# An output product whose second pass reuses the first pass's split weights, in a fused RWKV-7, pooling and MLP decoder step

## The chip, the core and the metric

The kernel runs on one NeuronCore of a Trainium2 chip. The metric is the device time of one execution in microseconds, from the program's start to its end; 1776.5 us is the median of three runs before the change (1774.28 to 1776.87). Engines are written as the profile writes them: PE is the matrix engine and PEld its weight load, DVE the vector engine, ACT the scalar engine, POOL GpSimd, and SP the engine that only issues DMAs and semaphore operations here. DMAs are issued from the queues of SP, ACT and POOL, and each queue issues in order: a DMA that waits for data holds what stands behind it on that queue.

## What is computed

One layer of a decoder trunk over 1088 tokens (1024 of a prompt, 8 sequences of 8), with 1024 features. Cut to what matters here:

```python
h = rms_norm(x, norm_mix) * (1 + sc) + sh            # sc, sh, gt = silu(c) @ w_ada_mix + b
P = h @ w_in
o_r = rwkv7_branch(P[:, :1792]); o_p = pool_branch(P[:, 1792:2304])
g_r, g_p = split(sigmoid(P[:, 2304:]))
merged = g_r * (o_r @ w_br_rwkv) + g_p * (o_p @ w_br_pool)     # the branch sums
x = x + gt * (merged @ w_out)                                   # the output product
sh, sc, gt = split(silu(c) @ w_ada_mlp + b_ada_mlp)             # the mixer's conditioning
h = rms_norm(x, norm_mlp) * (1 + sc) + sh
x = x + gt * (square(relu(h @ w_ff1)) @ w_ff2)                  # the channel mixer
y = rms_norm(x, norm_final)
```

## The kernel before

Features lie on the 128 partitions and tokens along the free dimension: a row tile is 128 x 1088, and the 1024 features are eight such rows. The tokens are cut into three chunks of 364, 362 and 362 (CH); the first two together are 726 columns (CUT).

**Products in three parts.** Every product is made in a reduced-precision format (fp32r) from values split into a high and a low part: `mm3` multiplies high by high, high weight by low input, low weight by high input, all into one PSUM tile. So each weight half, 128 x 512 elements, has to be split as well. `weights` (L157) does this: it loads the raw half into one of two `wraw` buffers with a DMA on SP (L164), copies it to `whi` with rounding on ACT (L167), and subtracts on DVE or, for every second half, on POOL, to make `wlo` (L168). In phase 2 there are four buffers each for `whi` and `wlo` (two in the pool wp, two in p2), and weight halves are requested four ahead.

**Jobs and recording.** A `Job` is one output row of 128 features: it has weight halves, chunks, PSUM tags and a `consume` function that takes each PSUM tile off. `products` walks through the jobs in the order of a list. PE executes exactly in the order in which instructions are recorded. `Pace` decides this order: its clock advances by an estimate for each matmul recorded, the product stream is the background, and generators such as the norm or the conditioning are in front; a generator yields a number (so many ns of that clock later) or a condition. On ACT, DVE, POOL and SP the order is that of a list scheduler, which follows the dependencies, the number of buffers, and its own estimates of time.

**Phase 2** is what the change touches. In the order of recording:

- *Branch sums*, eight jobs `or_job` (L1238): one half each, all three chunks. `begin` loads two rows from DRAM scratch on ACT's queue: `t` (the gate, L1244) and `u` (the other branch's product, L1245). `consume` multiplies the gate with PSUM on DVE (L1246); `after` adds `u` on POOL (L1250), copies the high part on ACT (L1253), and makes the low part on DVE (L1254) into the tiles `ma` (726 columns) and `mb` (362). `t` and `u` share four buffers.
- *Residual rows*: `x_load` (L1264) loads the eight rows of x into `hx` buffers with DMAs on ACT's queue (L1268). It stands behind the branch sums in the list, but its loads depend only on free buffers.
- *Output product*, two passes of eight jobs `out_job` (L1271) with two halves each: the first pass over the first two chunks, the second over the third. Each pass loads and splits all 16 halves of `w_out`. `consume` is `residual` (L1428): it adds gate times PSUM to the residual row on DVE (L1433), and for the sample tokens with a second DVE operation and one on POOL (L1436, L1438).
- *The mixer's conditioning*, `ada` (L1232), a generator in front: three groups of `ada_part` (L239), each of which loads eight weight tiles of 512 KB (`hid`, four buffers, DMA on SP, L249), multiplies them on PE in four groups 7000 ns of the clock apart, and spreads the result. The first group comes 15000 + 7000 ns after the start of phase 2.
- *The mixer's norm*, `norm2` (L1278), another generator: it starts when `ada` is done. For each pass it squares the updated residual rows on ACT (L1290), adds them on DVE (L1292), takes statistics on PE (`stats`, PSUM tag wc), spreads the inverse root (`rms`), and scales the rows (L1303 to L1310, using DVE, ACT and POOL) into `ma` and `mb` again. Its temporary rows come from the four `t` buffers. The statistics are recorded 3500 ns after the seventh and the eighth output job of a pass.
- *The mixer*, `ff1_job` and `ff2_jobs`: the first three ff1 jobs run on the first two chunks as soon as the first pass is normed, then on the third chunk, and the rest on all three.

The `hx` pool has 16 row buffers. In phase 2 they hold, in turn, the branches' inputs, then the residual rows and the mixer's hidden rows.

## Time and profile before

| | |
|---|---|
| median of three runs | 1776.5 us (1774.28 to 1776.87) |
| profiled execution | 1773.06 us, span of its instructions 1771.3 us |
| PE / DVE / ACT / POOL busy | 1690.8 / 853.1 / 556.0 / 243.3 us |
| granted clock of PE, mean | 0.983 |
| moved to and from HBM | 138.64 MB read, 38.84 MB written |

The profile comes from one execution. Times in its rows are microseconds from the start of the span. A row of the timeline gives start, duration, engine, line, operation, the names of what is written and read, shape and count of merged instructions; in brackets stands how long the engine had been idle before it and what released it. L148 is the line of the helper that records every matmul, so the names of its tiles tell the products apart: `mm<-hx` and `w<-hx` belong to the branches, `mm<-ma` and `w<-mb` first to the output product and later to the mixer, `wc<-hid` to the conditioning, `wc<-kct,t` to the statistics. L168 is the split of a weight half. A group's row gives the count, then busy time and mean ns of one, then the idle time before it.

### The profile page before, as it was taken

The page shows a single profiled execution, that of the slowest core. Times are in us where ns is not written, and L with a number is a line of the kernel's source. Part 1 is how long each engine was busy: PE and PEld are TensorE (multiplying, and loading weights), DVE is VectorE, ACT ScalarE, POOL GpSimd, SP SyncE. Part 2 cuts the span into 40 slices and gives each one's busy share as a digit, 9 for nine tenths or more (in the row PEclk, how much of TensorE's full clock was granted, in tenths as well). Part 3 has the DMA queues.
Part 4 walks back from the last instruction along what each step waited for, and adds up shares of the span by engine and source line. Part 5 has one row for each costly group of instructions (what it writes and reads, how often), then busy time and mean ns, then how long its engine had stood idle before and what let it go on. Part 6 is the DMA issues. An engine that isn't in the chain of part 4 may idle for free.

```text
span 1771.3 us, 32564 instructions
## 1 busy us (share of the span) xinstructions
PE 1690.8 (95%) x13705; PEld 1581.4 (89%) x13705; DVE 853.1 (48%) x1566; ACT 556.0 (31%) x1116; POOL 243.3 (14%) x315
## 2 busy tenths in 40 slices
PE   5899999989999999998999999999999999999997
PEld 2889878877888798888889899999999999999996
DVE  5575557735673637343535742433333343323346
ACT  4433343444334334221224630303121222212132
POOL 0110101000000000002413511110111111111111
PEclk9999999989999999999999999999999999999998
DMA  8214314222413241848742221111111111111112
GB/s 334 103 64 141 136 46 152 73 93 79 135 65 116 90 138 51 319 159 321 280 168 73 83 66 48 42 48 43 47 43 42 49 42 47 43 48 42 42 42 102
DMA packets 80083, 179.61 MB, mean 101 GB/s; under 512 B 16480, under 2 KB 23136, under 8 KB 79936
## 3 DMA queue, kind: packets, MB, share of 16 engines
q1 hardware_dynamic: 72128, 156.66, 26.0%
q10 hardware_dynamic: 7664, 20.42, 3.4%
q8 instruction: 108, 1.77, 0.4%
q0 software_dynamic: 144, 0.44, 0.1%
q14 instruction: 39, 0.32, 0.1%
HBM read 138.64 MB, written 38.84 MB: 100 GB/s over the span
## 4 chain that ended last, share of the span: by engine, by line
PE 87%; DVE 6%; DMA 3%; ACT 2%; issue 2%; POOL 0%; DVEq 0%; SPq 0%; ACTq 0%; POOLq 0%
PE mm L148 58%; PE w L148 24%; PE wc L148 4%; PE w L155 1%; DMA t<-d_th 1%; DMA hx<-in_xT 1%; DVE wlo L168 0%; DVE sq L365 0%; DMA x<-in_xT 0%; DVE hv L762 0%; DVE ma L1305 0%; DMA wt<-d_x 0%; DMA aw<-in_w_ada_mix 0%; DVE hx L1423 0%; DMA hid<-in_w_ada_mlp 0%
## 5 line engine op out<-in xcount | busy, mean ns | idle before, releaser
L148 PE MATMUL mm<-hx,whi 128*128 128x362 f32 (+2 forms) x2608 | 684.3, 344 | 8.4 <-DVE t L1246 5.8
L148 PEld LDWEIGHTS mm<-hx,whi 128*128 128x128 f32 x2608 | 458.8, 192 | 44.4 <-issue 24.6
L148 PE MATMUL mm<-hx,wlo 128*128 128x362 f32 (+3 forms) x1304 | 430.8, 330 | 2.7 <-DVE wlo L168 2.7
L167 ACT ACTIVATE whi<-wraw 128x512 fp32r<-128x512 f32 x246 | 155.2, 631 | 543.6 <-PE w L148 360.1
L148 PE MATMUL mm<-ma,whi 128*128 128x364 f32 (+1 forms) x1280 | 319.1, 330 | 0.8 <-DVE ma L1254 0.5
L148 PEld LDWEIGHTS mm<-hx,wlo 128*128 128x128 f32 x1304 | 250.6, 192 | 3.4 <-DVE wlo L168 3.3
L148 PEld LDWEIGHTS mm<-ma,whi 128*128 128x128 f32 x1280 | 227.0, 189 | 8.1 <-issue 5.9
L168 DVE TENSOR_TENSOR wlo<-wraw,whi 128x512 fp32r<-128x512 f32 x157 | 115.0, 733 | 215.7 <-ACT whi L167 207.4
L148 PE MATMUL mm<-ma,wlo 128*128 128x364 f32 (+1 forms) x640 | 211.0, 330 | 0.2 <-DVE wlo L168 0.2
L168 POOL TENSOR_TENSOR wlo<-wraw,whi 128x512 fp32r<-128x512 f32 x89 | 118.1, 1327 | 658.5 <-ACT whi L167 658.5
L1433 DVE SCALAR_TENSOR_TENSOR hx<-mm,aq,hx 128x364 f32<-128x364 f32 (+4 forms) x136 | 74.7, 587 | 206.4 <-PE mm L148 206.3
L148 PE MATMUL w<-mb,whi 128*128 128x362 f32 x640 | 157.9, 328 | 0.9 <-DVE rs L1436 0.6
L148 PEld LDWEIGHTS mm<-ma,wlo 128*128 128x128 f32 x640 | 121.0, 189 | 0.5 <-DVE wlo L168 0.5
L148 PEld LDWEIGHTS w<-mb,whi 128*128 128x128 f32 x640 | 112.9, 189 | 1.5 <-issue 0.8
L1327 DVE TENSOR_TENSOR ft<-ft 128x362 f32<-128x362 f32 (+1 forms) x96 | 53.0, 575 | 127.2 <-ACT ft L1326 126.8
L148 PE MATMUL w<-mb,wlo 128*128 128x362 f32 x320 | 104.8, 328 | 1.5 <-DVE wlo L168 1.3
L148 PE MATMUL w<-hx,whi 128*128 128x362 f32 x416 | 102.9, 328 | 0.0
L148 PE MATMUL mm<-hid,whi 128*128 128x364 f32 (+4 forms) x304 | 75.3, 330 | 0.0
L148 PEld LDWEIGHTS w<-hx,whi 128*128 128x128 f32 x416 | 73.1, 189 | 0.8 <-issue 0.8
L1326 ACT ACTIVATE ft<-mm 128x364 f32<-128x364 f32 x64 | 29.3, 474 | 128.1 <-PE mm L148 128.0
L148 PE MATMUL w<-hx,wlo 128*128 128x362 f32 x208 | 67.4, 324 | 0.0
L148 PEld LDWEIGHTS w<-mb,wlo 128*128 128x128 f32 x320 | 60.6, 189 | 2.1 <-DVE wlo L168 2.1
(301 smaller groups left out, 2088.4 us busy)
## 6 DMA issues: line engine op xcount, KB each, us to landing
wraw<-in_w_ff SPq DMA_DIRECT2D x134, 256.0 KB, 2.6
wraw<-in_w_in SPq DMA_DIRECT2D x68, 256.0 KB, 2.9
hid<-in_w_ada_mlp SPq DMA_DIRECT2D x24, 512.0 KB, 5.3
d_th<-px SPq DMA_DIRECT2D x22, 544.0 KB, 3.1
wt<-d_x SPq DMA_DIRECT2D x20, 544.0 KB, 4.3
t<-d_th ACTq DMA_DIRECT2D x16, 544.0 KB, 6.5
aw<-in_w_ada_mix SPq DMA_DIRECT2D x16, 512.0 KB, 6.8
wraw<-in_w_out SPq DMA_DIRECT2D x32, 256.0 KB, 2.7
```

The source lines that it names most:

```text
L148: return self.nc.tensor.matmul(out, lhsT, rhs, **kw)
L155: self.nc.tensor.transpose(out, in_, ident)
L167: nc.scalar.activation(hi, raw, AF.Copy)
L168: (nc.gpsimd if n % 2 and n >= self.solo else nc.vector).tensor_tensor(lo, raw, hi.bitcast(F32), op=ALU.subtract)
L1326: nc.scalar.activation(t[:, :n], ps[:, :n], AF.Relu)
L1327: nc.vector.tensor_tensor(t[:, :n], t[:, :n], t[:, :n], op=ALU.mult)
L1433: nc.vector.scalar_tensor_tensor(x[:, c0:c0 + m], ps[:, :m], gt[:, 0:1], x[:, c0:c0 + m], op0=ALU.mult, op1=ALU.add)
```

## The change

Three things change in phase 2.

1. *Weights of the output product.* In the first pass the halves of the jobs 0 to 3 are split as before, and both parts are also stored to DRAM scratch (`d_w`) by DMAs on SP. The halves of the jobs 4 to 7 are split into `hx` buffers by a new function, always on DVE, and stay there. The second pass runs over the jobs in the order 4, 5, 6, 7, 0, 1, 2, 3: the first four use the parts kept, the last four load both parts back from DRAM into `whi` and `wlo`. Nothing of `w_out` is split a second time. `norm2` follows the same order in its second pass.
2. *Residual rows.* Instead of `x_load`, each branch job loads one residual row at its end. A one-column copy on POOL from the job's sum into the row (`behind`) makes the load wait for that sum. The halved gate that `x_load` also made is made ahead of the jobs.
3. *Conditioning.* `ada` starts when branch job 1 is recorded, its first two tiles wait for that job's sum through `behind`, and the lead before its first group is 12000 instead of 15000.

```diff
@@ weights @@
-    def weights(self, src):
+    def weights(self, src, keep=None):
...
+        if keep is not None:
+            for t, s in ((hi, keep[:, 0:512]), (lo, keep[:, 512:1024])):
+                nc.sync.dma_start(s, t.bitcast(F32))
...
+    def split(self, t, src):
+
+        nc = self.nc
+        raw = self.wp.tile([P, 512], F32, tag="wraw", bufs=WB[0], name=self.nm("wraw"))
+        nc.sync.dma_start(raw, src)
+        hi, lo = t[:, 0:512], t[:, 512:1024]
+        nc.scalar.activation(hi, raw, AF.Copy)
+        nc.vector.tensor_tensor(lo, raw, hi.bitcast(F32), op=ALU.subtract)
+        return [(hi[:, q * 128:(q + 1) * 128], lo[:, q * 128:(q + 1) * 128]) for q in range(4)]
+
+    def weights_again(self, src):
+
+        n = self.nw
+        self.nw += 1
+        wp, x = (self.p2, "x") if n % 4 > 1 else (self.wp, "")
+        hi = wp.tile([P, 512], F32R, tag="whi" + x, bufs=WB[1], name=self.nm("whi"))
+        lo = wp.tile([P, 512], F32R, tag="wlo" + x, bufs=WB[1], name=self.nm("wlo"))
+        for t, s in ((hi, src[:, 0:512]), (lo, src[:, 512:1024])):
+            self.nc.sync.dma_start(t.bitcast(F32), s)
+        return [(hi[:, q * 128:(q + 1) * 128], lo[:, q * 128:(q + 1) * 128]) for q in range(4)]
...
@@ stream @@
-                W[id(j), h] = self.weights(j.halves[h])
+                w = j.halves[h]
+                W[id(j), h] = w() if callable(w) else self.weights(w)
...
@@ run @@
+            self.d_w = scratch("d_w", 8)
...
@@ phase2 @@
+        def behind(x):
+
+            nc.gpsimd.tensor_copy(x[:, 0:1], self.mark[:, 0:1])
+            return x
+
         def ada():
             asb = self.row(p, "R", 1, w=9 * 128)[:, :512]
+            yield lambda: ("or_job", 1) in self.done
+            first = [behind, behind]
+
+            def tile():
+                t = self.row(p, "hid", 4)[:, :1024]
+                return first.pop()(t) if first else t
+
             for g in range(3):
-                yield from self.ada_part("w_ada_mlp", g, lambda: self.row(p, "hid", 4)[:, :1024], asb, self.aq, "b_mlp", (8 * g, 8 * g + 4), 7000, 3000, 15000 if g == 0 else 0)
+                yield from self.ada_part("w_ada_mlp", g, tile, asb, self.aq, "b_mlp", (8 * g, 8 * g + 4), 7000, 3000, 0 if g else 12000)
...
+                self.mark = t
+                x = HX(F32)
+                self.xr.append(x)
+                nc.scalar.dma_start(behind(x), io["xT"][m])
+                self.done.add(("or_job", m))
...
-        def x_load():
-            nc.vector.tensor_scalar(gt, self.am[:, 16:24, :], 0.5, None, op0=ALU.mult)
-            for m in range(8):
-                self.xr.append(HX(F32))
-                nc.scalar.dma_start(self.xr[m], io["xT"][m])
-            yield
+        nc.vector.tensor_scalar(gt, self.am[:, 16:24, :], 0.5, None, op0=ALU.mult)
+        kept = {}
+        again = (4, 5, 6, 7, 0, 1, 2, 3)
+
+        def out_half(m, i, h):
+            src, put = io["w_out"][m][:, h * 512:(h + 1) * 512], self.d_w[2 * (m % 4) + h]
+            if i:
+                return kept[m, h] if m > 3 else self.weights_again(put)
+            if m < 4:
+                return self.weights(src, put)
+            kept[m, h] = self.split(HX(), src)
+            return kept[m, h]
...
-            return Job([io["w_out"][m][:, h * 512:(h + 1) * 512] for h in range(2)], lambda: self.residual(self.xr[m], gt[:, m, :]), ch,
+            return Job([lambda h=h: out_half(m, i, h) for h in range(2)], lambda: self.residual(self.xr[m], gt[:, m, :]), ch,
...
@@ norm2 @@
-                for m in range(8):
+                for n, m in enumerate(again if i else range(8)):
                     yield lambda: ("out", m, i) in self.done
-                    t = T() if m else acc
+                    t = T() if n else acc
                     nc.scalar.activation(t[:, a:b], self.xr[m][:, a:b], AF.Square)
-                    if 0 < m < 7:
+                    if 0 < n < 7:
                         nc.vector.tensor_tensor(acc[:, a:b], acc[:, a:b], t[:, a:b], op=ALU.add)
-                    if m > 5:
+                    if n > 5:
                         yield 3500
-                        self.stats(po, acc if m == 6 else t, bl, m == 6, m == 7)
+                        self.stats(po, acc if n == 6 else t, bl, n == 6, n == 7)
...
@@ the list @@
-        order += [(x_load, 0)]
         for i in range(2):
-            for m in range(8):
+            for m in again if i else range(8):
                 order += U(out_job(m, i))
```

## The prediction

> **What bounds the kernel now.** I read the page first, then busy time by stretch around the output product, then the rows of the engines inside those stretches. The page:
>
> ```profile
> span 1771.3 us, 32564 instructions
> ...
> PE 1690.8 (95%) x13705; PEld 1581.4 (89%) x13705; DVE 853.1 (48%) x1566; ACT 556.0 (31%) x1116; POOL 243.3 (14%) x315
> ```
>
> TensorE (PE) is the bound almost everywhere, so what can be won is PE idle time, and no edit removes a matmul. Busy time by stretch, branch sums to mixer (columns: stretch, its length, then busy time and count on PE, weight load, DVE, ACT, POOL, then granted clock, DMA share, GB/s):
>
> ```profile
> 803.00:818.00 15.00, 15.00 (x92) 14.75 (x90) 2.21 (x4) 1.90 (x3) 2.21 (x2) 1.00 1.00 369
> 818.00:824.00 6.00, 0.19 (x2) 0.17 (x2) 0.82 (x2) 0.00 (x0) 0.36 (x1) 0.70 1.02 410
> 824.00:859.00 35.00, 35.00 (x206) 31.80 (x207) 20.59 (x30) 9.73 (x17) 17.82 (x9) 0.95 0.92 325
> 859.00:877.00 18.00, 17.16 (x106) 14.48 (x106) 12.81 (x15) 5.75 (x10) 9.67 (x4) 1.00 0.79 280
> 877.00:940.00 63.00, 63.00 (x391) 55.51 (x389) 20.00 (x29) 15.74 (x23) 9.02 (x7) 1.00 0.43 144
> 940.00:986.00 46.00, 40.38 (x249) 38.58 (x247) 32.93 (x48) 24.32 (x40) 21.53 (x18) 1.00 0.27 86
> ```
>
> PE is idle for 5.81 us in the second row, 0.84 us in the fourth (18.00 - 17.16) and 5.62 us in the last (46.00 - 40.38). The PE rows that place this:
>
> ```profile
> 807.48 0.50 PE L148 MATMUL mm<-hx,whi 128*128 128x364 f32 x2
> ...
> 808.97 0.49 PE L148 MATMUL mm<-hx,whi 128*128 128x364 f32 x2
> ...
> 823.86 0.95 PE L148 MATMUL mm<-hx,whi 128*128 128x364 f32 x2 [5.81 <-DVE t L1246]
> 824.60 0.51 PE L148 MATMUL mm<-hx,wlo 128*128 128x364 f32 x1
> ...
> 827.30 0.33 PE L148 MATMUL mm<-hx,wlo 128*128 128x364 f32 x1
> ...
> 835.99 1.06 PE L148 MATMUL wc<-hid,sT 128*32 128x512 f32 x8
> ...
> 866.87 0.49 PE L148 MATMUL mm<-ma,whi 128*128 128x364 f32 x2
> ...
> 939.94 0.96 PE L148 MATMUL wc<-kct,R 128*128 128x18 f32 x8
> ...
> 981.86 0.49 PE L148 MATMUL mm<-ma,whi 128*128 128x364 f32 x2
> 982.59 0.43 PE L148 MATMUL mm<-ma,wlo 128*128 128x364 f32 x1 [0.24 <-DVE wlo L168]
> 986.21 0.83 PE L148 MATMUL wc<-kct,t 128*128 128x3 f32 x6 [3.19 <-DVE t L1292]
> ```
>
> Nine matmuls take 1.49 us (807.48 to 808.97), so a branch job of 36 takes 5.96 and the first began at 806.0. After the 5.81 us wait the clock is low: nine take 2.70 (824.60 to 827.30), 1.2 too many, and the two before them 0.74 (823.86 to 824.60), 0.4 too many. The first output pass begins at 866.87, the conditioning's last group runs at 939.94; the mixer's product begins at 981.86 and stands at 986.21 for the second statistics. The chain of waits says why the first wait is there:
>
> ```profile
> 803.49 9.14 DMA hx<-in_xT
> ...
> 812.65 10.43 DMA t<-d_th
> ```
>
> The branch sums' first row is issued when a residual row has landed and takes 10.43 us behind them.
>
> **The change, part by part. Residual rows.** They go behind the sums, one per job, so the first four sum rows meet empty queues. I take the 5.81 us and the 1.6 of slow clock after it as gone: PE needs job 0's row used by job 2's start, at 817.9. After its matmuls a sum takes these steps:
>
> ```profile
> 823.18 0.98 DVE L1246 SCALAR_TENSOR_TENSOR t<-t,mm 128x364 f32<-128x364 f32 x2 [8.01 <-DMA t<-d_th]
> ```
>
> ```profile
> 825.70 2.51 POOL L1250 TENSOR_TENSOR t<-t,t 128x1088 f32<-128x1088 f32 x1 [7.33 <-DMA t<-d_th]
> ```
>
> ```profile
> 828.24 0.81 ACT L1253 ACTIVATE ma<-t 128x726 fp32r<-128x726 f32 x1 [11.24 <-POOL t L1250]
> ```
>
> ```profile
> 875.48 0.92 DVE L1254 TENSOR_TENSOR ma<-t,ma 128x726 fp32r<-128x726 f32 x1 [3.24 <-ACT ma L1253]
> ```
>
> With a third piece of 0.5 and handovers of 0.1 to 0.2 that is 5.9 us. The ten POOL copies that order the loads are one column wide; no row shows one. They lie between 0 and the 2.51 us of the 1088 columns, in width far nearer to 0, and POOL was busy for 17.8 of 35 us: nothing. Behind such a load on ACT stands the split of the same sum's last third, which waits for the same POOL addition; I take nothing, and at most 2.5 us on the last sum, which other loads outweigh below.
>
> What the move may cost is bandwidth later. Issues from 795 to 880 (count, size, median us to landing), the landing times of all sum rows, and a weight half:
>
> ```profile
> t<-d_th ACTq DMA_DIRECT2D x16, 544.0 KB, 6.5
> hid<-in_w_ada_mlp SPq DMA_DIRECT2D x14, 512.0 KB, 6.7
> hx<-in_xT ACTq DMA_DIRECT2D x8, 544.0 KB, 9.7
> ```
>
> ```profile
> DMA to landing us min/median/max: 2.7/3.9/10.4
> ```
>
> ```profile
> wraw<-in_w_out SPq DMA_DIRECT2D x32, 256.0 KB, 2.7
> ```
>
> From the first sum (806.0 + 5.96 + 1.5 + 2.5 = 816) to the moment at which the addition of job 7 needs its second row (806.0 + 8 x 5.96 + three conditioning groups of 1.1 + 1.5 = 859) the new order moves 12 sum rows (6.7 MB), 6 residual rows (3.3), 10 conditioning tiles (5.2), 9 weight halves (2.4) and 8 new stores of splits (2.1): 19.7 MB in 43 us. The cover: a second row is asked for when the sum two jobs before it is split, 6.4 us after that job's end, and used two jobs later plus 1.5, so 7.5 us after the request; it takes 2.7 to 3.9 unloaded, and some 3.5 are spare. The last sum is needed only by the fourth block of the first pass's second half, 7 us in, and takes 5.9: 1 us more. So the stall that comes back is S = 19.7 MB / rate - 47.5 us: 0.5 at 410 GB/s (818-824), 5.9 at 369 (803-818), 13.1 at 325 (824-859). I take 410 and round to S = 1: there all queues were full, while the 325 is near what was asked for (2.2 MB per job of (866.87 - 823.86) / 6 = 7.2 us is 306).
>
> The Trainium skill (DMA: Bandwidth & Descriptors, Specifications) gives about 358 GB/s from HBM per core; by that figure S would be 7.5 and the change a loss of 2 us. This trace disagrees, with 410 GB/s while PE waited, so the sum is made without it.
>
> **Conditioning later.** It now waits for job 1, then 12 + 7 instead of 15 + 7 us of recorded PE work: 2 x 5.96 + one step of 0.5 + 19 - 22 = 9.4 us later in PE's order. The matmuls are the same. But the mixer's norm is recorded behind its last group, and that group is not 9.4 later on the clock: the waits ahead of it go, 5.81 + 1.6 + 0.84 = 8.25. So 939.94 becomes 941.1 + S, and everything of the norm shifts by 1.15 + S.
>
> **Second pass on kept weights.** Eight halves stay in SBUF; eight are stored as two 256 KB parts each in the first pass and read back. The 16 stores are 4.2 MB; half of them are in S, the rest falls where 144 GB/s were moved: nothing. SP issues them behind the splits that its next weight load waits for anyway, and four buffered halves of 4 us cover that. Four splits go from POOL to DVE, which is busy for 20 of 63 us there: nothing. A half read back (two parts) takes between 2.7 us and twice that, against three halves of 2.0 us ahead of it: hidden. If it is late, the wait in the next part covers up to 8 us.
>
> **What DVE then does.** Rows of DVE and POOL in the second pass, and groups of both from 956.4 to 986.2:
>
> ```profile
> 956.44 2.75 DVE L1303 SCALAR_TENSOR_TENSOR t<-hx,g,t 128x726 f32<-128x726 f32 x3 [1.62 <-ACT t L302]
> ...
> 959.70 2.01 DVE L1305 SCALAR_TENSOR_TENSOR ma<-t,aq,ma 128x726 fp32r<-128x726 f32 x1
> ...
> 962.20 0.96 DVE L1305 SCALAR_TENSOR_TENSOR ma<-t,aq,ma 128x726 fp32r<-128x726 f32 x1
> ...
> 972.36 0.68 DVE L168 TENSOR_TENSOR wlo<-wraw,whi 128x512 fp32r<-128x512 f32 x1
> ...
> 983.48 2.68 DVE L1292 TENSOR_TENSOR t<-t,t 128x362 f32<-128x362 f32 x3
> ```
>
> ```profile
> 959.58 1.36 POOL L168 TENSOR_TENSOR wlo<-wraw,whi 128x512 fp32r<-128x512 f32 x1 [3.25 <-ACT whi L167]
> ```
>
> ```profile
> L168 POOL TENSOR_TENSOR wlo<-wraw,whi 128x512 fp32r<-128x512 f32 x5 | 7.9, 1581 | 7.2 <-ACT whi L167 7.2
> ```
>
> ```profile
> L168 DVE TENSOR_TENSOR wlo<-wraw,whi 128x512 fp32r<-128x512 f32 x6 | 5.6, 939 | 0.1
> ...
> L1433 DVE SCALAR_TENSOR_TENSOR hx<-w,gt,hx 128x298 f32<-128x298 f32 x6 | 3.1, 516 | 0.0
> ...
> L1436 DVE TENSOR_TENSOR rs<-w,gt 128x64 f32<-128x64 f32 x6 | 1.3, 210 | 0.0
> ```
>
> From 956.44 to 986.16 DVE works without a break on the norm's rows, the splits, the residuals and the second statistics' sums: this, not PE, sets 986.21. A DVE operation beside a POOL split takes 2.01 instead of 0.96. Five splits on DVE (a sixth begins at the very end) and five on POOL lie in there. Of these the second pass's go, and the first four of the mixer's product move in (their buffers come free earlier), two on each engine: 3 x 0.68 + 3 x 1.05 = 5.2 us less. Two residuals (0.73 each) fall before the chain, as the pass begins some 10 us earlier: 1.5. So 29.7 becomes 23.0 (bounds 29.7, none saved, and 16.3, twice as much saved), and DVE ends at 956.44 + 1.15 + 23.0 = 980.6 + S. PE is there at 983.0 - 8.25 - 2.4 (the last stretch's other gaps) = 972.3 + S and waits 8 us.
>
> **Sum:** 986.2 - 980.6 - S = 5.6 - 1 = 4.6 us. Profiled execution 1773.06 - 4.6 = 1768.5; its span is 1.8 below that time, and it is 3.4 below the median of 1776.5. Against the median: **1772**.
>
> **Rivals.** (a) *PE-bound*: if DVE's sums for the second statistics slip in earlier, or the chain loses twice what I say, PE sets the end: 986.2 - 972.3 - 1 = 12.9 us gained, 1763.6. For it: DVE is idle for two thirds of 877-940. Against: the sums need row buffers that the norm's rows hold.
> (b) *The transfer comes back*: at 369 GB/s S is 5.9 and eats the gain: 1776.8. For it: this is what full queues moved in 803-818.
> (c) *Slower*: the last branch sum becomes the bound. If the mix of residual rows, conditioning tiles and stores runs at the 325 GB/s of 824-859, S is 13.1, PE waits inside the first output pass, the later conditioning pushes the norm back with it, and the time is 7.5 longer: 1784. It loses over 0.2% (3.55 us) from S = 9.2, that is below 347 GB/s. Against: 410 was seen. The skill's 358 lies between (b) and (c).
> (d) *The splits were not what held DVE*: the chain stays at 29.7 and only shifts: 1.15 + S later, 1778.6.
>
> **How the numbers follow.** My forecast has 0.46, of which 0.40 gains over 0.2% (about what a measurement of this kernel can tell) and 0.06 less; (a) 0.16; (b) 0.16; (c) 0.14; (d) 0.08, a quarter of it slower. Faster 0.40 + 0.16 = 0.56; same 0.06 + 0.16 + 0.06 = 0.28; slower 0.14 + 0.02 = 0.16. The forecast's own range is 1769 to 1775; with (a), (b) and (d) 1764 to 1779, leaving out most of (c).
>
> **What would show it.** Right: no wait at the third branch job; the conditioning's last group near 942; no split of output weights on POOL or DVE in the second pass; a wait of some 8 us of PE for line L1292's sums at about 981. Wrong: a stall near the seventh branch sum of over 3 us, PE waiting for weights read back ahead of the norm, or no wait for the second statistics.

## The result, and the profile after

The kernel after takes 1786.94 us (median of five runs, 1779.54 to 1789.31) beside 1776.5 for the kernel before (five runs, 1772.69 to 1776.87): a ratio of 1.0053 with a 95% interval of 1.0028 to 1.0078. Measured a second time, it took 1784.66 (six runs) beside 1775.14 (eleven), 1.0047 (1.0031 to 1.0064). It is slower by half a per cent, 9.5 to 10.4 us between the medians; 4.6 us of gain were forecast.

From the page of the kernel after:

```profile
span 1785.1 us, 32528 instructions
...
PE 1698.9 (95%) x13705; PEld 1588.8 (89%) x13705; DVE 841.2 (47%) x1562; ACT 546.1 (31%) x1100; POOL 227.7 (13%) x313
...
HBM read 138.64 MB, written 43.04 MB: 102 GB/s over the span
```

The matmuls are the same, DVE and POOL do 12 and 16 us less, and 4.2 MB more are written: the stores. The profiled execution took 1786.94 us, its span is 13.8 us longer than before. Of these 6.3 us lie ahead of the first branch job, which starts at 806.0 before and 812.32 after and up to which nothing was changed (the last section shows where they come from); 7.5 lie behind it. I read the profile from that job on. PE's waits from there to the second statistics, kernel after (engine, line, whom it waited for; sum, times, longest):

```profile
PE mm L148 <- ACT ma L1291: 9.4, 2, 8.6
PE wc L148 <- DVE t L1341: 8.1, 1, 8.1
PE mm L148 <- DVE ma L1292: 1.3, 2, 1.0
```

These are all. The 5.81 us at the third branch job are gone, and so are the waits on splits in the second pass. In their place stand 10.7 us on the split of the last two branch sums, 8.9 of them on the last, and the forecast wait for the second statistics. The rows of PE's timeline that carry them:

```profile
871.88 0.44 PE L148 MATMUL mm<-ma,whi 128*128 128x364 f32 x1 [0.76 <-ACT ma L1291]
873.31 0.44 PE L148 MATMUL mm<-ma,whi 128*128 128x364 f32 x1 [0.99 <-DVE ma L1292]
...
883.05 0.67 PE L148 MATMUL mm<-ma,whi 128*128 128x364 f32 x1 [8.64 <-ACT ma L1291]
884.00 0.67 PE L148 MATMUL mm<-ma,whi 128*128 128x364 f32 x1 [0.28 <-DVE ma L1292]
...
962.40 0.96 PE L148 MATMUL wc<-kct,R 128*128 128x18 f32 x8
...
1003.20 1.44 PE L148 MATMUL wc<-kct,t 128*128 128x3 f32 x6 [8.13 <-DVE t L1341]
```

The wait of 8.64 us is inside the first output pass, at the block that needs the last branch sum. The last conditioning group runs at 962.40, 150.1 us after the first branch job (939.94 - 806.0 = 133.9 before). The chain of waits tells what the sum waited for:

```profile
850.68 9.16 DMA wraw<-in_w_out
...
860.33 9.07 DMA wraw<-in_w_out
...
869.48 10.04 DMA t<-d_th
...
879.68 2.49 POOL t L1288
...
882.19 0.82 ACT ma L1291
```

Three transfers of 256 to 544 KB in a row, each of 9 to 10 us. The second sum row of the last job is issued when a weight half has landed, lands 67 us after the first branch job, and then come the addition and the split as the prediction had them.

Why the sum row stands behind a weight half, though it is issued on another queue and goes to another buffer, can be read from the semaphores in the trace. This program's DMAs on SP's and ACT's queues share eight semaphores, and a DMA is issued only when the earlier one with the same semaphore has landed: of some 8900 such pairs in the 17 profiles none is otherwise, and there are never more than eight of these DMAs under way. The sum row's semaphore was that of the weight half that landed at 869.40 (860.33 + 9.07); the row was issued 0.08 us later, as one of eight under way.

Busy time by stretch (columns as in the prediction):

```profile
812.32:828.32 16.00, 16.00 (x98) 16.00 (x98) 5.82 (x12) 3.52 (x6) 5.27 (x4) 1.00 0.74 236
...
871.00:884.00 13.00, 2.33 (x8) 1.27 (x8) 4.79 (x8) 2.95 (x6) 3.94 (x3) 0.63 1.03 404
...
822.30:879.50 57.20, 50.35 (x303) 44.89 (x301) 26.58 (x40) 14.19 (x24) 25.84 (x21) 0.96 1.00 381
...
874.39:891.46 17.07, 8.15 (x29) 7.75 (x29) 4.08 (x8) 2.65 (x4) 3.93 (x3) 0.50 0.79 298
```

In the first 16 us the DMA engines are only 0.74 busy and move 236 GB/s. Then, from 10 us after the first branch job until the last sum row has landed, they are full: 57.2 us at 381 GB/s, 21.8 MB. The last row is the clock: it stays at half from 874.39 to 891.46, 8.4 us beyond the end of the wait, and the matmuls there take twice their time.

For all kernels below the stretch from the first branch job to the end is taken apart in the same way. *Waits* are PE's idle stretches of over 0.15 us up to the last conditioning group (`wc<-kct,R` on L148), *clock* is half of PE's busy time in stretches at half clock, *work* is what is left. *Norm* is the time from that group to the second statistics (`wc<-kct,t ... x6`), *rest* from there to the end. All in us, each from one profile.

| kernel | last group at | = waits | + clock | + work | norm | rest | sum | first branch job at |
|---|---|---|---|---|---|---|---|---|
| before | 133.9 | 6.6 | 1.7 | 125.6 | 46.3 | 785.1 | 965.3 | 806.0 |
| after | 150.1 | 10.7 | 4.1 | 135.3 | 40.8 | 781.9 | 972.8 | 812.3 |
| after_again | 150.9 | 10.5 | 4.4 | 136.0 | 40.8 | 782.9 | 974.6 | 812.5 |
| after_five | 152.5 | 12.8 | 4.4 | 135.2 | 40.8 | 782.0 | 975.3 | 804.8 |
| x_only | 133.3 | 4.8 | 3.1 | 125.4 | 46.3 | 785.9 | 965.5 | 804.3 |
| w_only | 139.5 | 9.7 | 4.5 | 125.3 | 40.4 | 784.0 | 964.0 | 808.4 |
| a_only | 143.2 | 5.5 | 1.7 | 136.1 | 43.4 | 782.0 | 968.7 | 800.2 |
| xw | 135.5 | 6.7 | 2.8 | 126.0 | 40.4 | 784.7 | 960.7 | 805.0 |
| no_store | 146.5 | 6.2 | 4.8 | 135.5 | 43.4 | 782.7 | 972.6 | 805.9 |
| joint | 146.3 | 7.5 | 3.7 | 135.1 | 41.5 | 783.4 | 971.2 | 806.4 |
| joint_again | 146.6 | 7.3 | 4.2 | 135.0 | 41.5 | 783.7 | 971.8 | 805.5 |
| xsplit | 143.7 | 5.3 | 3.2 | 135.2 | 40.8 | 782.8 | 967.3 | 805.8 |
| xlate_wa | 140.1 | 2.3 | 3.2 | 134.6 | 40.8 | 782.8 | 963.7 | 802.9 |
| xlate | 126.2 | 0.6 | 0.0 | 125.6 | 46.3 | 785.8 | 958.2 | 807.8 |
| xlate_w | 132.7 | 4.3 | 2.9 | 125.5 | 40.4 | 784.0 | 957.2 | 814.9 |
| xlate_w_five | 130.1 | 2.5 | 1.7 | 125.9 | 40.4 | 784.3 | 954.9 | 810.1 |
| best | 141.0 | 9.8 | 4.8 | 126.4 | 41.1 | 782.4 | 964.5 | 804.3 |

Two columns hardly vary within a kind. *Work* is 125.3 to 126.4 with the conditioning at its old place and 134.6 to 136.1 with it later; *norm* is 40.4 to 41.5 with all output weights kept, and with all or half of them split again it is 46.3 with the conditioning at its old place and 43.4 with it later (a_only, no_store). So kept weights alone shorten it by 5.9 us (w_only), the later conditioning alone by 2.9, and both together by 5.5. What differs most is waits and clock.

### The profile page after: what moved, and what is told of

Read it like the earlier page. It is cut to its first block, busy times and chain, and to the rows that moved or that the text cites. A ratio compares the mean times of both kernels' runs of the same rounds, so it can differ in the third digit from the quotient of the medians.

```text
span 1785.1 us, 32528 instructions
## 1 busy us (share of the span) xinstructions
PE 1698.9 (95%) x13705; PEld 1588.8 (89%) x13705; DVE 841.2 (47%) x1562; ACT 546.1 (31%) x1100; POOL 227.7 (13%) x313
## 4 chain that ended last, share of the span: by engine, by line
PE 85%; DMA 5%; DVE 5%; ACT 3%; issue 2%; POOL 1%; SPq 0%; DVEq 0%; ACTq 0%; POOLq 0%
PE mm L148 56%; PE w L148 24%; PE wc L148 4%; DMA wraw<-in_w_out 2%; DMA t<-d_th 1%; PE w L155 1%; DMA x<-in_xT 1%; DMA wt<-d_x 0%; DVE hv L787 0%; DMA aw<-in_w_ada_mix 0%; DVE hx L1471 0%; DMA wraw<-in_w_br 0%; POOL t L1288 0%; DVE tt L789 0%; ACT whi L167 0%
## 5 line engine op out<-in xcount | busy, mean ns | idle before, releaser
L148 PE MATMUL mm<-hx,whi 128*128 128x362 f32 (+2 forms) x2608 | 687.0, 345 | 2.4 <-DVE hx L419 1.1
L148 PEld LDWEIGHTS mm<-hx,whi 128*128 128x128 f32 x2608 | 460.8, 192 | 38.0 <-issue 17.7
L148 PE MATMUL mm<-hx,wlo 128*128 128x362 f32 (+3 forms) x1304 | 432.5, 332 | 2.7 <-DVE wlo L168 2.7
L148 PE MATMUL mm<-ma,whi 128*128 128x364 f32 (+1 forms) x1152 | 289.6, 332 | 10.7 <-ACT ma L1291 9.4
L167 ACT ACTIVATE whi<-wraw 128x512 fp32r<-128x512 f32 x222 | 140.0, 631 | 488.7 <-PE w L148 355.2
L148 PEld LDWEIGHTS mm<-hx,wlo 128*128 128x128 f32 x1304 | 251.6, 193 | 3.4 <-DVE wlo L168 3.3
L148 PEld LDWEIGHTS mm<-ma,whi 128*128 128x128 f32 x1152 | 206.4, 191 | 15.3 <-ACT ma L1291 10.0
L168 DVE TENSOR_TENSOR wlo<-wraw,whi 128x512 fp32r<-128x512 f32 x145 | 101.8, 702 | 198.7 <-ACT whi L167 191.6
L148 PE MATMUL mm<-ma,wlo 128*128 128x364 f32 x576 | 190.8, 331 | 0.0
L168 POOL TENSOR_TENSOR wlo<-wraw,whi 128x512 fp32r<-128x512 f32 x77 | 100.6, 1307 | 612.6 <-ACT whi L167 612.6
L148 PE MATMUL w<-mb,whi 128*128 128x362 f32 x576 | 142.1, 327 | 0.1
L1376 DVE TENSOR_TENSOR ft<-ft 128x362 f32<-128x362 f32 (+1 forms) x96 | 52.4, 570 | 132.4 <-ACT ft L1375 132.4
L148 PEld LDWEIGHTS mm<-ma,wlo 128*128 128x128 f32 x576 | 109.8, 191 | 0.0
L148 PE MATMUL w<-hx,whi 128*128 128x362 f32 x416 | 102.6, 328 | 0.0
L148 PEld LDWEIGHTS w<-mb,whi 128*128 128x128 f32 x576 | 101.9, 189 | 0.4 <-POOL mb L1359 0.4
L148 PE MATMUL w<-mb,wlo 128*128 128x362 f32 x288 | 94.2, 327 | 0.0
L148 PE MATMUL mm<-hid,whi 128*128 128x364 f32 (+4 forms) x304 | 75.4, 330 | 0.0
L148 PEld LDWEIGHTS w<-hx,whi 128*128 128x128 f32 x416 | 72.8, 189 | 0.8 <-issue 0.8
L1486 POOL TENSOR_TENSOR hx<-hx,rs 128x64 f32<-128x64 f32 x72 | 36.8, 512 | 255.4 <-DVE rs L1484 255.3
L148 PE MATMUL w<-hx,wlo 128*128 128x362 f32 x208 | 67.2, 323 | 0.0
```

The source lines that it names most:

```text
L148: return self.nc.tensor.matmul(out, lhsT, rhs, **kw)
L167: nc.scalar.activation(hi, raw, AF.Copy)
L168: (nc.gpsimd if n % 2 and n >= self.solo else nc.vector).tensor_tensor(lo, raw, hi.bitcast(F32), op=ALU.subtract)
L1376: nc.vector.tensor_tensor(t[:, :n], t[:, :n], t[:, :n], op=ALU.mult)
L1486: nc.gpsimd.tensor_tensor(x[:, NPR:NT], x[:, NPR:NT], t, op=ALU.add)
```

## The experiments

Where the expectation of xlate puts the last conditioning group at some 148 us, it took the last rows named `wc<-kct,R` ahead of the second statistics, which are the spread of the first statistics (L155), 15.4 to 15.9 us behind that group in every kernel; its interval of 30.7 to the second statistics is the 46.3 of the table. Differences between kernels are the same by both.

**The three parts, each alone, and two together.** The first takes back the weights and the conditioning, the second the residual rows and the conditioning, the third the residual rows and the weights, the fourth the conditioning alone. The edits against the kernel after, in this order: weights, conditioning, residual rows.

```diff
-            if i:
-                return kept[m, h] if m > 3 else self.weights_again(put)
...
+            return self.weights(src)
-        again = (4, 5, 6, 7, 0, 1, 2, 3)
+        again = tuple(range(8))
```

```diff
-            yield lambda: ("or_job", 1) in self.done
-            first = [behind, behind]
...
+            tile = lambda: self.row(p, "hid", 4)[:, :1024]
...
-... 7000, 3000, 0 if g else 12000)
+... 7000, 3000, 0 if g else 15000)
```

```diff
-                nc.scalar.dma_start(behind(x), io["xT"][m])
...
+        order += [(x_load, 0)]
```

Residual rows alone:

> The kernel before with the residual rows behind the branch sums and nothing else of the change. Theory (crowding: the last branch sum is late because everything that is moved until its second row lands, 25.6 MB in the changed kernel, goes at about 400 GB/s): the wait of 5.8 us at the third branch job goes, but the residual rows now lie between the sums' rows, so PE waits inside the first output pass: against the changed kernel 2.6 MB of stores less and two conditioning tiles (1 MB) more, so 12 us less 4, some 6 to 8 us. The time comes out within 3 us of before. Rival (the stores of splits alone hold up the sums' rows): no wait over 2 us in the first output pass, and 5 to 7 us faster than before.

Weights alone:

> The kernel before with the second pass on the first's split weights and nothing else. Theory: the 5.8 us at the third branch job stay; the stores (2 MB ahead of the last sum) lengthen the wait of 0.8 us in the first output pass to some 4 us; the second pass has no splits, so VectorE's chain of norm rows gets 5 to 6 us shorter and the wait of 3.2 us for the second statistics goes. Time between 3 us faster and 1 us slower than before. Rival (the splits were not what held VectorE): the wait for the second statistics stays at 3 us or grows, and the time is 3 us or more slower.

Conditioning alone:

> The kernel before with the conditioning recorded later and nothing else. Theory: with the first wait only shortened (three conditioning tiles fewer among the residual rows, 5.8 us to some 3), the 9.4 us later in PE's order reach the norm, and the wait for the second statistics grows from 3.2 to 10 us or more; 4 to 8 us slower than before. Rival (the norm has slack, its order does not matter): the wait for the second statistics stays under 5 us and the time is that of before or 2 us less.

Residual rows and weights, without the conditioning:

> The changed kernel with the conditioning as before. Theory: the wait in the first output pass is as long as in the changed kernel or longer (10 to 14 us, two more conditioning tiles ahead of the last sum), but the norm comes 9.4 us earlier in PE's order, so the 8.1 us for the second statistics fall to under 2: some 8 us less than the changed kernel in the part from the first branch job on, near the time of before. Rival (the later conditioning was harmless and what it takes off the queues early on is worth more): no faster than the changed kernel.

Measured, on one chip beside 31 runs of before (1774.18), ten runs each: x_only 1768.39, ratio 0.9973 (0.9958 to 0.9988); w_only 1772.38, 0.999 (0.9975 to 1.0005); a_only 1774.03, 1.002 (0.9995 to 1.0045); xw 1768.51, 0.997 (0.9953 to 0.9986). So the parts that were to gain do not lose, and the kernel without the conditioning's move is faster than before: that move turns 0.997 into 1.005.

Against the expectations: w_only came out as its theory said (first wait 5.8 us, 3.8 at the last sums, *norm* 5.9 shorter), except that 1.3 us of the wait for the second statistics stay. In a_only the first wait fell as forecast, but the wait for the second statistics is 9.0 and not 10, phase 2 is 3.4 us longer and not 4 to 8, and the interval of its ratio holds 1. In x_only the last sum costs 4.1 us and not 6 to 8, and the median is 5.8 us below that of before, forecast within 3. In xw the wait in the first output pass is 5.8 us and not 10 to 14, so the tiles at their old place make it shorter and not longer. PE's rows of xw at the last branch sum and the second statistics:

```profile
873.80 0.67 PE L148 MATMUL mm<-ma,whi 128*128 128x364 f32 x1 [4.45 <-ACT ma L1285]
...
980.91 0.83 PE L148 MATMUL wc<-kct,t 128*128 128x3 f32 x6 [1.28 <-DVE t L1335]
```

and the rows by stretch, first 16 us and from 10 us to the last sum row, of xw:

```profile
805.00:821.00 16.00, 16.00 (x98) 16.00 (x98) 2.74 (x6) 2.04 (x4) 5.30 (x4) 1.00 0.92 343
...
815.00:868.30 53.30, 51.37 (x315) 45.16 (x313) 25.02 (x37) 13.65 (x23) 26.90 (x18) 1.00 1.00 386
```

of x_only:

```profile
814.30:866.30 52.00, 51.37 (x318) 45.77 (x317) 26.27 (x40) 14.27 (x24) 27.20 (x18) 1.00 0.99 374
```

With its tiles at their old place the conditioning uses the first 16 us (343 GB/s beside 236), and PE's product waits 6.7 us in all instead of 10.7. The residual rows remove the first wait also when alone, but 4.1 us come back at the last branch sum: the sum of the stretch, 965.5, is that of before. Its ten runs are faster than before all the same, by 0.27%; the profiled one (1771.52) is among the slower of them, and one profile doesn't show where that gain lies.

**No stores.** The jobs 0 to 3 are split again in the second pass; the jobs 4 to 7 stay kept.

```diff
-                return kept[m, h] if m > 3 else self.weights_again(put)
+                return kept[m, h] if m > 3 else self.weights(src)
...
-                return self.weights(src, put)
+                return self.weights(src)
```

> The changed kernel without the stores: the halves of the jobs 0 to 3 are loaded and split again in the second pass, those of 4 to 7 are kept as in the change. Theory: 2.6 MB fewer ahead of the last sum at 380 GB/s, so the wait in the first output pass falls from 10.7 to some 4 us; the eight splits that return lengthen VectorE's chain by 2 to 3 us, so the wait for the second statistics is 9 to 11 us; the part from the first branch job on falls from 973 to about 967 us. Rival (stores are not what crowds): the wait stays at 9 us or more.

Measured: 1778.61, ratio 1.0036 (1.002 to 1.0051; ten runs beside 19 of before). Waits fall from 10.7 to 6.2, norm rises from 40.8 to 43.4: the stores cost some 4.5 us of waits and bring 2.6 in the norm. Of the 6 us that the theory had for phase 2 nothing is left (972.6 for 972.8): clock and rest take up the remaining difference, 0.7 and 0.8. From 10 us to the last sum row it is

```profile
815.90:868.30 52.40, 50.31 (x303) 44.85 (x301) 26.86 (x40) 14.41 (x24) 27.28 (x21) 1.00 0.98 369
```

52.4 us x 369 GB/s = 19.3 MB, 2.5 MB below the kernel after, at a slightly lower rate.

**Fewer, and more, transfers for the same bytes.** In one kernel both parts of a stored half are one tile and one DMA of 512 KB, stored and read back (the edit puts both parts of every other weight half into one tile too); in the other each residual row comes by two DMAs.

```diff
-                nc.sync.dma_start(s, t.bitcast(F32))
+                nc.sync.dma_start(keep[:, 0:1024], both.bitcast(F32))
```

> The changed kernel with both parts of a split half in one tile, so that a half is stored and read back by one DMA of 512 KB instead of two of 256 KB: the same bytes, five DMAs fewer ahead of the last branch sum. Theory (bytes at the rate of full queues): the wait in the first output pass stays within 2.5 us of the 10.7 us of the changed kernel. Rival (the number of DMAs: each issue waits until an earlier one has landed, and the stores fill the places): the wait falls by half or more.

> The kernel with one DMA per stored half once more. If 7.5 us was chance, the wait in the first output pass is 9 to 12 us here; if the number of DMAs counts, it is 6 to 8.5 us again.

```diff
-                nc.scalar.dma_start(behind(x), io["xT"][m])
+                behind(x)
+                for a, b in ((0, 544), (544, NT)):
+                    nc.scalar.dma_start(x[:, a:b], io["xT"][m][:, a:b])
```

> The changed kernel with each residual row loaded by two DMAs of half the columns: the same bytes, six to seven DMAs more ahead of the last sum. Theory (bytes): the wait in the first output pass is that of the changed kernel, 9 to 12 us. Rival (the number of DMAs, which the kernel with stores of both parts in one DMA left open, 7.5 us instead of 10.7): 13 us or more.

One execution each: joint 1779.42 and, again, 1779.06 with waits of 7.5 and 7.3 us; xsplit 1774.9 with 5.3. Joint lies between its theory and its rival, its repeat shows that this was not chance, and xsplit is below both of its forecasts. The kernel after, once more:

> The changed kernel once more, for the spread of its waits between executions. Theory: the waits come from the order and the bytes, so the wait in the first output pass is again 9 to 12 us, that for the second statistics 7 to 9; the half-clock stretches ahead of the first branch job fall elsewhere, so that job starts anywhere between 800 and 814 us. Rival (the slower first part belongs to the changed program): it starts at 812 us again, with the half-clock stretches at the same places, 250 and 263 and 424 and 434.

It took 1788.88, with waits of 10.5 and its first branch job at 812.5, as the rival had it; the third profile of this program, below, is the one that differs. So the same bytes with fewer, larger transfers had a shorter stall, and with more, smaller ones too: the number of DMAs alone doesn't set it. For xsplit the trace shows less ahead of the last sum row: when that was issued, 3 stores and 9 conditioning tiles had been issued since the first branch job, in the kernel after 6 and 10. In joint it was the bytes of 6 stores and 10 tiles as well. There the last row was issued 2.3 and 3.2 us earlier than in the kernel after, counted from the first branch job, and 1.2 and 0.6 us after the landing that it depends on, where all three profiles of the kernel after have 0.1 us or less: fewer DMAs, each of which needs one of the eight semaphores, no longer hold it. That this is the whole of the 3 us is not shown, since the edit also changes the tiles.

**Residual rows behind the last sum.** All eight are issued when the last branch job is done, with the conditioning later and at its old place:

```diff
+                if m == 7:
+                    for k in range(8):
+                        self.xr.append(HX(F32))
+                        nc.scalar.dma_start(behind(self.xr[k]), io["xT"][k])
```

> The changed kernel with all eight residual rows behind the last branch sum instead of one behind each. Theory: 3.9 MB fewer ahead of the last sum's second row, 10 us at 380 GB/s, so the wait in the first output pass falls from 10.7 to under 2 us; the 8 us for the second statistics stay (the conditioning's place in PE's order is the same); from the first branch job on some 960 us instead of 973. Rival (the residual rows cost nothing there, or a residual row is now late for the first output job): a wait of 4 us or more in the first pass.

> The same with the conditioning as in the kernel before, so kept weights and late residual rows only. Theory: neither wait: under 2 us in the first output pass, and under 3 us for the second statistics, since the norm comes 9.4 us earlier in PE's order; from the first branch job on 953 to 956 us, that is 9 to 12 us faster than the kernel before. Rival (conditioning tiles loaded early crowd the first sums instead): a wait of 3 us or more at the branch jobs, and no more than 5 us gained.

Measured beside 19 runs of before (1773.82): xlate_wa 1772.62, 0.9988 (0.997 to 1.0005); xlate_w 1759.32, 0.9916 (0.9896 to 0.9936). With the six residual rows that had been issued ahead of the last sum row (3.3 MB) out of the crowd, the waits of the changed kernel fall from 10.7 to 2.3 us, and the loss is gone; with the conditioning at its old place too, it is the fastest kernel of this study. Both came out a little above their theories in phase 2: 963.7 us for 960, and 957.2 for 953 to 956, where 3.6 us of wait stay at the last sum. Of the five runs of xlate_w the profiled one (1773.91) is the slowest by 14 us, with its first branch job at 814.9.

**A denser conditioning** on top of it, started later but with shorter steps (lead 31500, steps 5500):

> Kept weights, residual rows behind the last branch sum, and a conditioning that loads its first four tiles at once, begins 15 us later and then goes in steps of 5.5 instead of 7 us, so that it ends 1.5 us earlier in PE's order. Theory: one or two pairs of tiles leave the crowded stretch, so the wait of 3.6 us in the first output pass falls to 0 to 2; the norm comes 1.5 to 4 us earlier and the wait for the second statistics is gone; from the first branch job on 951 to 955 us, 10 to 14 us less than the kernel before. Rival (the denser steps now wait for their tiles): a wait of 2 us or more at a conditioning group, and no better than 957.

Measured: 1773.93, ratio 1.0001 (0.9987 to 1.0015). PE's rows from the first group on:

```profile
857.38 1.05 PE L148 MATMUL wc<-hid,sT 128*32 128x512 f32 x4 [0.37 <-DMA hid<-in_w_ada_mlp]
...
872.88 1.89 PE L148 MATMUL wc<-kct,R 128*128 128x18 f32 x8 [4.60 <-ACT R L280]
...
895.58 0.43 PE L148 MATMUL mm<-ma,wlo 128*128 128x364 f32 x1 [1.01 <-DVE wlo L168]
...
918.20 0.60 PE L148 MATMUL mm<-ma,hx 128*128 128x364 f32 x2 [2.19 <-ACT hx L180]
```

and what ACT does ahead of the wait of 4.60 us:

```profile
865.08 6.58 ACTq L1293 DMA_DIRECT2D hx<-in_xT  x6
871.71 0.63 ACT L167 ACTIVATE whi<-wraw 128x512 fp32r<-128x512 f32 x1 [6.59 <-DMA hx<-in_xT]
872.25 0.58 ACT L280 ACTIVATE R<-wc 128x512 f32<-128x512 f32 x1
```

Nothing is won. The wait at the last branch sum is gone and 0.5 us stay at the second statistics, as the theory had it, but what this saves PE now waits elsewhere, 9.8 us up to the last group. Less than half a microsecond of it is for a conditioning tile. The largest part, 4.6 us, is the first group's result: ACT has to copy it (L280) and stands for 6.6 us issuing six residual rows, the last four of them each held until an earlier DMA has landed. That is a price of issuing all the rows at one place on ACT's queue, and the rival, a wait of over 2 us at a conditioning group, was right in its number but not in its reason. Nearly all of the rest are splits of weight halves.

**What was left.** Three kernels on one chip, six runs each: the kernel after, xlate_w, and the residual rows behind the last sum with nothing else changed.

> The kernel after the change, once more, beside xlate_w_five and before on one chip. Theory (the loss is that of phase 2 alone): the stretch from the first branch job to the end was 972.8 and 974.6 us in two profiles against 965.3 before, so the median is 7.5 to 9.3 us above the median of before, a ratio of 1.0042 to 1.0052, and the wait at the last branch sum is 9.8 to 10.7 us. Rival (this program also loses some 6 us ahead of the first branch job, as both profiles so far had it at 812.3 and 812.5 against 806.0): the first branch job starts near 812.4 again and the ratio is 1.0075 to 1.009. Second rival (the change is not slower, the first result was a draw of the clock): a ratio below 1.002.

> Kept and stored weights, all residual rows behind the last branch sum, conditioning as before, once more, beside after_five on the same chip. Theory (what the order of work in phase 2 gives): from the first branch job to the end 957.2 us against 965.3, so 8 us below before, 1766, a ratio of 0.9955; the ratio of 0.9916 seen before held a favourable draw of the clock ahead of phase 2. Rival (this program's first part is truly shorter as well): the first branch job starts at 800 to 803, the median is 1759 to 1761, a ratio of 0.991 to 0.9925.

> Residual rows alone, all eight behind the last branch sum; output weights split in both passes and the conditioning as before. Theory (the weights kept shorten DVE's chain by 5.9 us and the norm ends the path): the last conditioning group falls some 148 us after the first branch job, PE resumes at the second statistics 30.7 us later, at 179, so from the first branch job to the end 963 to 965 us and a ratio of 0.998 to 1.000, some 6 us above xlate_w_five. Rival (where the residual rows stand makes all of the gain, the weights none): 957 to 958 us and the time of xlate_w_five within 2 us.

Measured beside 1775.14 (eleven runs): after_five 1784.66, 1.0047 (1.0031 to 1.0064); xlate_w_five 1762.94, 0.9922 (0.9906 to 0.9939); xlate 1765.14, 0.9944 (0.9927 to 0.996). PE's waits up to the second statistics, of after_five:

```profile
PE mm L148 <- ACT ma L1291: 10.1, 2, 9.4
PE wc L148 <- DVE t L1341: 8.1, 1, 8.1
PE mm L148 <- DVE t L1284: 1.4, 1, 1.4
PE mm L148 <- DVE ma L1292: 1.3, 2, 1.0
```

and of xlate_w_five:

```profile
PE mm L148 <- ACT ma L1285: 2.0, 1, 2.0
PE wc L148 <- DVE t L1336: 1.3, 1, 1.3
PE mm L148 <- DVE ma L1286: 0.5, 1, 0.5
```

and PE's rows of xlate:

```profile
870.55 0.44 PE L148 MATMUL mm<-ma,whi 128*128 128x364 f32 x1 [0.56 <-DVE ma L1286]
...
980.28 1.44 PE L148 MATMUL wc<-kct,t 128*128 128x3 f32 x6 [3.18 <-DVE t L1331]
```

After_five bears out the theory that the loss is phase 2's own: the first branch job starts at 804.8 this time, and the ratio is the one that phase 2 alone gives; the interval leaves out both rivals. The wait at the last two sums is 11.4 us, a little over the forecast. Xlate_w_five came out at the rival's ratio but not for its reason, since its profile has the first branch job late, at 810.1; phase 2 itself gave 10.4 us (965.3 - 954.9); where the rest of the 12.2 between the medians lies, one profile doesn't tell. Of xlate the theory was wrong by 5 us. The norm takes the 46.3 that it said, but the last conditioning group falls at 126.2 and not at 133, because the wait at the last branch sum and the slow clock behind it are nearly gone (0.6 and 0.0). So the rival nearly came true: most of the gain of the fastest kernel is the place of the residual rows. The kept weights add 3.3 us in phase 2 (958.2 - 954.9) and 2.2 in the medians, which the intervals of the two ratios don't tell apart: 5.9 less in the norm and 1.5 less in the rest, against 1.9 more of waits, 1.7 of clock and 0.3 of work.

## Why the prediction was wrong

The sum of the prediction, term by term, against two profiles (us, from the table):

| term | predicted | after | after_five |
|---|---|---|---|
| conditioning later in PE's order | +9.4 | +9.7 | +9.6 |
| waits and slow clock of before gone | -8.25 | -8.3 | -8.3 |
| S, the stall at the last branch sum (measured: all waits up to the last group) | +1 | +10.7 | +12.8 |
| slow clock behind that stall | 0 | +4.1 | +4.4 |
| DVE's chain in the norm | -6.7 | -5.5 | -5.5 |
| rest | 0 | -3.2 | -3.1 |
| phase 2 | -4.6 | +7.5 | +9.9 |
| ahead of the first branch job | 0 | +6.3 | -1.2 |

In after_five 11.4 of the 12.8 us are at the last two branch sums; in after all 10.7 are.

**The step that failed is S.** The mechanism and the place were forecast: S = bytes / rate - 47.5, a stall at the last branch sum inside the first output pass, which the prediction also named as a sign of being wrong. The size was wrong, 1 us for 10.7, in both of its factors. The rate was 381 GB/s and not 410: full DMA engines for 57 us gave less than the 6 us from which I took the 410. And 21.8 MB were moved, not 19.7. By the formula the first alone makes S 4.2 (19.7 / 0.381 - 47.5). With both it is 57.2 - 47.5 = 9.7, which tests only the cover of 47.5, because rate and bytes are measured over these same 57.2 us; the cover held within 1 us. I had weighed the 325 GB/s away as what was asked for, rightly (the DMA share there was 0.92), but put the most favourable short row in its place.

Rival (c) is what happened in kind, and its 7.5 us are what phase 2 lost in the first profile, but that agreement is luck: (c) rested on 325 GB/s and an S of 13.1. At 381 GB/s and 19.7 MB its sum would still have left a gain of 1.4 us. The loss comes from the bytes and from the slow clock behind the stall, which no rival had.

The Trainium skill (DMA: Bandwidth & Descriptors, Specifications) gives about 358 GB/s, from which the prediction worked out a loss of 2 us. Over 57 us this trace shows 381, in 871 to 884 us 404, so the figure is too low here, though the loss worked out from it had the right sign. The Trainium skill (HBM Reference, Specifications) has about 425 for a core that streams alone; the highest row shown here is the 410 over 6 us.

**Where the bytes came from.** The prediction counted what is issued until the last sum needs its row: 12 sum rows, 6 residual rows, 10 conditioning tiles, 9 weight halves and 8 stores. Issued from 10 us after the first branch job until that row had landed were 12, 7, 12, 9 and 9. The row was under way for 10 us with full engines, and in that time the next tiles, a residual row and stores were issued beside it. The conditioning's move was priced by PE's order alone, and that price was right (9.7 us of work for 9.4). It also takes its tiles out of the first 16 us, where with the tiles at their old place 343 to 346 GB/s were moved (xw, x_only) and after the change 236, and puts them into the crowd; that was not priced. Xw against the kernel after shows it: 6.7 us of waits instead of 10.7.

**What hangs on a stall.** The clock behind a wait of 8.6 us was not in the sum: 4.1 us more, though I had charged 1.6 for the same thing where it was to go. And since the norm waits for the last conditioning group, all of this shifts the path to the end.

**Right.** The first wait and its slow clock went. DVE's chain is what sets the second statistics and became shorter, by 5.5 of 6.7 us. That the splits held it w_only shows, where kept weights alone bring 5.9, so rival (d) falls. But the 1.5 us that the prediction added for the conditioning's place don't add: alone it brings 2.9 (a_only), on top of the kept weights nothing. PE stands there for 8.13 us, forecast 8. No output weight is split in the second pass and none read back was waited for, though the eight parts took 3.5 and 3.7 us in the median:

```profile
whi<-d_w SPq DMA_DIRECT2D x4, 256.0 KB, 3.5
wlo<-d_w SPq DMA_DIRECT2D x4, 256.0 KB, 3.7
```

The copies that order the loads are small, 0.18 to 0.88 us each, as on POOL in the kernel after:

```profile
832.16 0.88 POOL L1260 COPY hx<-t 128x1 f32<-128x1 f32 x1
...
862.34 0.53 POOL L1260 COPY hx<-t 128x1 f32<-128x1 f32 x1
...
869.59 0.18 POOL L1260 COPY hx<-t 128x1 f32<-128x1 f32 x1
...
882.22 0.18 POOL L1260 COPY hx<-t 128x1 f32<-128x1 f32 x1
```

Rival (a) nearly came true where the conditioning stayed: in xw and xlate_w_five PE waits only 1.3 us for the second statistics. The *rest* became 3.2 us shorter after, and most of that is work moved and not saved: by the trace PE has done 18 matmuls more ahead of the second statistics, 2.6 us.

## What to carry to other kernels

In this kernel a stretch in which the DMA engines are full was a budget of bytes: moving a load out of one wait moved it into the next, and the price was (bytes until the last thing needed has landed) / (rate over as long a stretch) minus the cover. Take the rate from a long row, and count what is issued while the last thing is under way. When a step is moved, ask where its transfers ran before and whether that gap stays empty. Put the loads that are needed last behind those that end the path, here the residual rows behind the last sum (xlate_wa 0.999 against 1.005 for the kernel after), but look at what waits behind them on the queue that issues them. A stall costs its slow clock too: 4.1 and 4.4 us behind stalls of 8.6 and 9.4 us, none behind one of 0.56.

## What was not expected of the hardware

**The clock varies between executions of one program.** Ahead of the first branch job each engine of the kernels before and after executes the same instructions in the same order, and yet the first branch job of one and the same program started at 812.3, 812.5 and 804.8 us (after), or at 814.9 and 810.1 (xlate_w). Rows by stretch from the start to the first branch job, and of a piece in it, before:

```profile
0.00:806.00 806.00, 750.65 (x8024) 659.31 (x8025) 455.79 (x865) 309.75 (x649) 54.30 (x126) 0.98 0.38 128
...
249.70:270.30 20.60, 18.15 (x182) 13.56 (x181) 15.60 (x25) 9.35 (x21) 1.47 (x4) 1.00 0.19 62
```

after, with two stretches at half clock inside that piece, where before had none:

```profile
0.00:812.30 812.30, 757.39 (x8023) 664.92 (x8024) 456.12 (x865) 310.36 (x649) 54.91 (x126) 0.97 0.37 127
249.75:253.16 3.41, 3.41 (x18) 2.81 (x17) 0.28 (x1) 1.24 (x4) 0.00 (x0) 0.50 0.01 5
263.40:270.23 6.83, 6.83 (x34) 5.40 (x31) 6.74 (x12) 2.29 (x7) 0.32 (x2) 0.50 0.41 124
```

and after_five, the same program:

```profile
0.00:804.80 804.80, 748.81 (x8023) 658.13 (x8024) 455.85 (x865) 309.78 (x649) 54.18 (x126) 0.98 0.37 128
```

PE is idle for 55.4, 54.9 and 56.0 us; it is its busy time, at the same matmuls, that differs by 8.6 us. Half of its busy time in the stretches at half clock ahead of that job is 17.0 us before, 25.2 after and 15.8 in after_five; without it 732 to 734 us are left in all three. All such stretches inside a kernel are multiples of 3.41 us long (3.41, 6.83, 10.24, 13.65, 17.07). The Trainium skill (TensorE: Matmul & The Clock Gate, Part 1) has a free-running window of 3413 ns that decides the clock, so that the loss varies from run to run; these lengths agree, and so does the spread. The spread means that a difference of 6 us between two profiles of this kernel, 0.35%, can be nothing but that; the profiles are compared from the first branch job on for this reason.
